# Loading the first slice of X in whole rows, and closing slice 0 in another order, in a matmul backward kernel

## The chip, the cores and the metric

One core of a Trainium2 chip. The metric is the device time of one execution in microseconds (us); all executions below count as undisturbed (fast). Verdicts come with a 95% interval. A profile is of one execution: of the kernel before a further one. Its span (first to last instruction) is about 1.8 us shorter than the device time.

## The reference

```python
batch, m, k, n = 16, 512, 1024, 768        # float32 inputs
grad_weight = np.einsum('bmk,bmn->kn', input, grad_output)   # out: 1024 x 768, float32
```

Seen as two matrices X (8192 x 1024) and G (8192 x 768) it is out = X^T G, a sum over 8192 rows. The kernel takes them in 64 slices of 128 rows.

## The kernel before

Each slice costs TensorE twelve matmuls with 512 moving columns: part A (row groups 0 to 3 of the output, columns 0 to 511), part B (row groups 4 to 7, same columns) and part N (the last 256 columns, "narrow", in transposed form). Each part holds four PSUM banks while it is open. `ORDER` says up to which slice each part goes next, and `!` that its banks are then emptied into SBUF:

```python
ORDER = (
    "A1! N1 B2! N2 A2 N3! A3 B3 A4! B5 N5 B6! N7 A6 N8! A9! B10 N9 B12! N12! A12! "
    "B15 AB17! n17! AB26! n26! AB41! n41! AB47 A50! B50! N64!"
).split()
WARMUP = [512] * 9 + [128] * 3
```

Slice 0 comes as float32 by the hardware queues of SP and ACT and is rounded to bf16 by VectorE and ScalarE. All other slices come by the software queue of GpSimd, which rounds on the way:

```python
nc.sync.dma_start(out=gf[:, 0:NA], in_=G[0:P, 0:NA])      # NA = 512, P = 128
nc.scalar.dma_start(out=xf[:, 0:NA], in_=X[0:P, 0:NA])
nc.sync.dma_start(out=gf[:, NA:N], in_=G[0:P, NA:N])
nc.scalar.dma_start(out=xf[:, NA:K], in_=X[0:P, NA:K])
# ... (warm-up matmuls on a constant, sizes from WARMUP)
for s in range(1, S):
    gt = xg.tile([P, N], bf16, name="gt")
    xt = xg.tile([P, K], bf16, name="xt")
    nc.gpsimd.dma_start(out=gt, in_=G[s * P : (s + 1) * P, :])
    nc.gpsimd.dma_start(out=xt, in_=X[s * P : (s + 1) * P, :])
# ... (casts of slice 0, 256 columns each, alternating VectorE and ScalarE)
# at the end, for each row group k of the output:
W = NB if k < 6 else c1 - c0                               # NB = 256
for c in range(c0, c1, W):
    nc.sync.dma_start(out=OUT[:, k, c : c + W], in_=acc[:, k, c : c + W])
```

Of the kernel before, what the change touches and what calls it, by code (L numbers as in the profile page):

```python
# [8 lines left out]
P = 128  # L9
NA = 512  # L10
# [4 lines left out]


ORDER = (
    "A1! N1 B2! N2 A2 N3! A3 B3 A4! B5 N5 B6! N7 A6 N8! A9! B10 N9 B12! N12! A12! "
    "B15 AB17! n17! AB26! n26! AB41! n41! AB47 A50! B50! N64!"
).split()  # L20

WARMUP = [512] * 9 + [128] * 3
XBUFS = 42


# [1 line left out]
def kernel(  # L27
# [6 lines left out]
    nc = tc.nc  # L34
# [3 lines left out]
    B, M, K = input.shape  # L38
    _, _, N = grad_output.shape
    S = B * M // P  # L40
    KS = K // P
    NB = N - NA
# [3 lines left out]
    X = input.rearrange("b m k -> (b m) k")  # L46
# [15 lines left out]
    xs = [None] * S  # L62
# [7 lines left out]
    xf = head.tile([P, K], f32, name="xf")  # L70
    gf = head.tile([P, N], f32, name="gf")
    nc.sync.dma_start(out=gf[:, 0:NA], in_=G[0:P, 0:NA])
    nc.scalar.dma_start(out=xf[:, 0:NA], in_=X[0:P, 0:NA])
    nc.sync.dma_start(out=gf[:, NA:N], in_=G[0:P, NA:N])
    nc.scalar.dma_start(out=xf[:, NA:K], in_=X[0:P, NA:K])


    ones = nc.const_aps.tensor(1.0, (P, P), bf16)
    wps = psum.tile([P, NA], f32, name="bank7")
    for i, cols in enumerate(WARMUP):  # L80
        nc.tensor.matmul(  # L81
# [18 lines left out]
    g0 = head.tile([P, N], bf16, name="g0")  # L100
    gwide[0] = g0[:, 0:NA]
    gnarrow[0] = g0[:, NA:N]
    QX = 256

    def round_pair(dst, src, c):
        nc.vector.tensor_copy(out=dst[:, c : c + QX], in_=src[:, c : c + QX])  # L106
        nc.scalar.copy(out=dst[:, c + QX : c + 2 * QX], in_=src[:, c + QX : c + 2 * QX])  # L107

    round_pair(g0, gf, 0)
    round_pair(xs[0], xf, 0)  # L110
    nc.vector.tensor_copy(out=g0[:, NA:N], in_=gf[:, NA:N])
    round_pair(xs[0], xf, NA)

    def add_out(dst, src):
        nc.vector.tensor_add(out=dst, in0=src, in1=dst)  # L115
# [7 lines left out]
    def wide_mm(bank, k, s, start, stop, c0=0, c1=NA):  # L123
        nc.tensor.matmul(  # L124
            bank, xs[s][:, k * P : (k + 1) * P], gwide[s][:, c0:c1], start=start, stop=stop
        )
# [90 lines left out]
    for a in range(P // SQ):  # L217
        c = NA + a * NT * SQ
        nc.scalar.dma_start(
            out=rows_of[:, :, c : c + NT * SQ],  # L220
            in_=turned[a * SQ : (a + 1) * SQ].rearrange("p b r t -> p b (r t)"),
# [3 lines left out]
    for k in range(KS):  # L225
        slices = range(parts["A" if k < KS // 2 else "B"].done, S)
        pieces = [(0, NA)] if k < KS - 1 else [(0, 256), (256, 384), (384, NA)]
        for c0, c1 in pieces:
            name = free.pop(0)
            bank = psum.tile([P, NA], f32, name=name)[:, 0 : c1 - c0]  # L230
            for s in slices:
                wide_mm(bank, k, s, s == slices[0], s == slices[-1], c0, c1)
            add_out(acc[:, k, c0:c1], bank)
            free.append(name)
            W = NB if k < 6 else c1 - c0
            for c in range(c0, c1, W):
                nc.sync.dma_start(out=OUT[:, k, c : c + W], in_=acc[:, k, c : c + W])

# [29 lines left out]
```

## Time and profile before

| | before |
|---|---|
| median time of 3 runs | 176.31 us (176.06 to 176.32) |
| span of the profile | 174.5 us |
| TensorE busy | 98% of the span |
| slice 1 begins on TensorE | 8.15 us |

The lines that show what bounds the kernel stand in the prediction. The columns are start, duration, engine, line, operation, tiles and count, then the idle time ahead and what ended it.

Weight loads run ahead of the matmuls, so where a load waits the matmuls themselves stand still for 0.33 us less than the load, by the start times of the matmuls in the trace. The difference of 0.33 us is the same at all such places below.

### The profile page before, as it was taken

Reading aid. Unit: us, or ns where it says so; the run is one execution under the profiler, and the core shown is the slowest. Engines: PE = TensorE matmul, PEld = TensorE weight load, DVE = VectorE, ACT = ScalarE, POOL = GpSimd, SP = SyncE. Lnnn points to the kernel's source line nnn. Section 1 sums busy time; section 2 is a strip of 40 time slices with the busy share of each in tenths; the row PEclk is TensorE's granted clock in tenths of the full one; section 3 lists DMA queues with packets and bytes.
Section 4 is the critical chain, followed back from the end, with each engine's and each line's share of the span. In section 5 each row is a group of like instructions: output and inputs, shape, how many; then the busy total and the mean of one; then the engine's idle time right before and its main releaser. Section 6 shows DMA issues by size and latency. Waiting matters only on the chain.

```text
span 174.5 us, 2024 instructions
## 1 busy us (share of the span) xinstructions
PE 170.8 (98%) x808; PEld 78.2 (45%) x808; DVE 60.8 (35%) x100; ACT 5.6 (3%) x10; POOL 66.9 (38%) x130
## 2 busy tenths in 40 slices
PE   8999999999999999999999999999999999999993
PEld 3344444444444444444444444444444444444463
DVE  0555582882940039300000662200460003932122
ACT  3440000000000000000000000000000000000000
POOL 7444444444434444444444444444174300000000
PEclk9999999999999999999999999999999999999999
DMA  5999999999999999999999999999999990085633
GB/s 160 231 208 207 208 209 208 209 208 208 209 210 208 208 208 209 208 209 208 208 208 208 210 209 206 209 207 208 208 209 208 207 206 16 0 190 149 168 98 120
DMA packets 25192, 33.09 MB, mean 190 GB/s; under 512 B 6496, under 2 KB 16608, under 8 KB 25184
## 3 DMA queue, kind: packets, MB, share of 16 engines
q0 software_dynamic: 18144, 28.91, 90.6%
q1 hardware_dynamic: 2592, 2.49, 4.3%
q10 hardware_dynamic: 4448, 1.57, 4.0%
q8 instruction: 6, 0.10, 0.2%
q14 instruction: 2, 0.02, 0.0%
HBM read 58.72 MB, written 3.15 MB: 355 GB/s over the span
## 4 chain that ended last, share of the span: by engine, by line
PE 94%; DMA 4%; issue 0%; POOL 0%; DVE 0%; POOLq 0%
PE bank L124 63%; PE bank L131 31%; DMA xt<-in_input_dram 4%; POOL gt L93 0%; DVE acc L115 0%; POOLq L252 0%
## 5 line engine op out<-in xcount | busy, mean ns | idle before, releaser
L124 PE MATMUL bank<-gt,xt 128*128 128x512 bf16 (+2 forms) x532 | 111.0, 368 | 0.1
L124 PEld LDWEIGHTS <-xt 128*128 128x128 bf16 x532 | 50.8, 98 | 58.8 <-DMA xt<-in_input_dram 1.1
L115 DVE TENSOR_TENSOR acc<-bank,acc 128x512 f32<-128x512 f32 (+2 forms) x62 | 37.9, 667 | 73.5 <-PE bank L124 73.1
L131 PE MATMUL bank<-xt,gt 128*128 128x512 bf16 x252 | 56.2, 379 | 0.0
L94 POOL DMA_DIRECT2D xt<-in_input_dram x63 | 33.5, 531 | 41.3 <-DMA xt<-in_input_dram 38.3
L93 POOL DMA_DIRECT2D gt<-in_grad_output_dram x63 | 33.6, 533 | 29.4 <-DMA gt<-in_grad_output_dram 26.9
L131 PEld LDWEIGHTS <-gt 128*128 128x128 bf16 x252 | 24.6, 98 | 29.8
L115 DVE TENSOR_TENSOR acct<-bank,acct 128x512 f32<-128x512 f32 x24 | 15.7, 682 | 30.0 <-PE bank L131 29.9
L81 PE MATMUL bank<-const-bfloat16-1.0 128*128 128x512 bf16 (+1 forms) x12 | 4.3, 550 | 0.8 <-PEq L252 0.8
L119 DVE COPY acc<-bank 128x512 f32<-128x512 f32 x4 | 2.6, 684 | 1.5 <-PE bank L124 1.5
L81 PEld LDWEIGHTS <-const-bfloat16-1.0 128*128 128x128 bf16 x12 | 1.6, 144 | 3.2 <-issue 3.2
L175 DVE STREAM_TRANSPOSE turned<-acct 128x512 f32<-128x512 f32 x4 | 2.9, 714 | 0.1
L124 PE MATMUL bank<-g,x 128*128 128x512 bf16 x8 | 2.4, 430 | 0.0
L121 ACT COPY acc<-bank 128x512 f32<-128x512 f32 x4 | 2.1, 589 | 1.8 <-PE bank L124 1.8
L106 DVE CAST g<-gf 128x256 bf16<-128x256 f32 x1 | 0.3, 324 | 4.3 <-DMA gf<-in_grad_output_dram 4.3
L119 DVE COPY acct<-bank 128x512 f32<-128x512 f32 x2 | 1.3, 686 | 1.3 <-PE bank L131 1.3
L107 ACT ACT_TABLE_LOAD x1 | 1.3, 1283 | 1.7 <-PEq L252 1.7
L124 PEld LDWEIGHTS <-x 128*128 128x128 bf16 x8 | 0.8, 108 | 1.1 <-ACT x L107 0.3
L121 ACT COPY acct<-bank 128x512 f32<-128x512 f32 x2 | 1.1, 588 | 1.5 <-PE bank L131 1.5
L131 PE MATMUL bank<-x,g 128*128 128x512 bf16 x4 | 1.0, 379 | 0.0
L107 ACT CAST x<-xf 128x256 bf16<-128x256 f32 x2 | 0.8, 402 | 0.5 <-DMA xf<-in_input_dram 0.5
L106 DVE CAST x<-xf 128x256 bf16<-128x256 f32 x2 | 0.6, 287 | 0.3 <-DMA xf<-in_input_dram 0.3
(7 smaller groups left out, 1.5 us busy)
## 6 DMA issues: line engine op xcount, KB each, us to landing
xt<-in_input_dram POOLq DMA_DIRECT2D x63, 256.0 KB, 8.5
gt<-in_grad_output_dram POOLq DMA_DIRECT2D x63, 192.0 KB, 8.5
out_dram<-acc SPq DMA_DIRECT2D x13, 128.0 KB, 2.9
out_dram<-turned ACTq DMA_DIRECT2D x4, 256.0 KB, 3.4
xf<-in_input_dram ACTq DMA_DIRECT2D x2, 256.0 KB, 4.1
gf<-in_grad_output_dram SPq DMA_DIRECT2D x1, 256.0 KB, 3.6
out_dram<-acc SPq DMA_DIRECT2D x1, 256.0 KB, 2.0
gf<-in_grad_output_dram SPq DMA_DIRECT2D x1, 128.0 KB, 3.8
```

Of the source, the lines that this page charges most:

```text
L81: nc.tensor.matmul(wps[:, 0:cols], ones, nc.const_aps.tensor(1.0, (P, cols), bf16), start=True, stop=True,)
L93: nc.gpsimd.dma_start(out=gt, in_=G[s * P : (s + 1) * P, :])
L94: nc.gpsimd.dma_start(out=xt, in_=X[s * P : (s + 1) * P, :])
L106: nc.vector.tensor_copy(out=dst[:, c : c + QX], in_=src[:, c : c + QX])
L107: nc.scalar.copy(out=dst[:, c + QX : c + 2 * QX], in_=src[:, c + QX : c + 2 * QX])
L115: nc.vector.tensor_add(out=dst, in0=src, in1=dst)
L119: nc.vector.tensor_copy(out=dst, in_=src)
L121: nc.scalar.copy(out=dst, in_=src)
L124: nc.tensor.matmul(bank, xs[s][:, k * P : (k + 1) * P], gwide[s][:, c0:c1], start=start, stop=stop)
L131: nc.tensor.matmul(bank, gnarrow[s].rearrange("p (r t) -> p t r", t=NT)[:, t], xs[s][:, h * NA : (h + 1) * NA], start=start, stop=stop,)
L175: nc.vector.transpose(out=turned[:, h * hb : (h + 1) * hb, :, t], in_=dst.rearrange("p (b r) -> p b r", r=SQ),)
```

## The change

X of slice 0 comes in one transfer of whole rows (4 KB) rather than two of half rows, with wide and then narrow G beside it on the other hardware queue. Slice 0 is worked off in the order A, B, N rather than A, N and B later. The casts are cut so that the first weights are ready soonest, the warm-up is 0.32 us longer to meet the later start, and output row group 6 goes out in two pieces.

```diff
-    "A1! N1 B2! N2 A2 ...
+    "A1! B1 N1 B2! N2 A2 ...
-WARMUP = [512] * 9 + [128] * 3
+WARMUP = [512] * 10 + [128] * 2
-    nc.scalar.dma_start(out=xf[:, 0:NA], in_=X[0:P, 0:NA])
+    nc.scalar.dma_start(out=xf, in_=X[0:P, :])
     nc.sync.dma_start(out=gf[:, NA:N], in_=G[0:P, NA:N])
-    nc.scalar.dma_start(out=xf[:, NA:K], in_=X[0:P, NA:K])
 # ... cut: the old casts, 256 columns each
+    round_by("DVE", g0, gf, 0, 256)
+    round_by("ACT", g0, gf, 256, NA)
+    round_by("DVE", xs[0], xf, 0, P)
+    round_by("ACT", xs[0], xf, 2 * P, 4 * P)
+    round_by("DVE", xs[0], xf, P, 2 * P)
+    round_by("DVE", xs[0], xf, 4 * P, 6 * P)
+    round_by("ACT", xs[0], xf, 6 * P, 8 * P)
+    round_by("DVE", g0, gf, NA, N)
-            W = NB if k < 6 else c1 - c0
+            W = NB if k < 7 else c1 - c0
```

More of the change, by code (lines that the diff above doesn't have):

```diff
@@ L17 @@
 ORDER = (
-    "A1! N1 B2! N2 A2 N3! A3 B3 A4! B5 N5 B6! N7 A6 N8! A9! B10 N9 B12! N12! A12! "
+    "A1! B1 N1 B2! N2 A2 N3! A3 B3 A4! B5 N5 B6! N7 A6 N8! A9! B10 N9 B12! N12! A12! "
     "B15 AB17! n17! AB26! n26! AB41! n41! AB47 A50! B50! N64!"
 ).split()
-WARMUP = [512] * 9 + [128] * 3
+WARMUP = [512] * 10 + [128] * 2
 XBUFS = 42
@@ L102, with round_by @@
     gnarrow[0] = g0[:, NA:N]
-    QX = 256
-    def round_pair(dst, src, c):
-        nc.vector.tensor_copy(out=dst[:, c : c + QX], in_=src[:, c : c + QX])
-        nc.scalar.copy(out=dst[:, c + QX : c + 2 * QX], in_=src[:, c + QX : c + 2 * QX])
-    round_pair(g0, gf, 0)
-    round_pair(xs[0], xf, 0)
-    nc.vector.tensor_copy(out=g0[:, NA:N], in_=gf[:, NA:N])
-    round_pair(xs[0], xf, NA)
+    def round_by(engine, dst, src, c0, c1):
+        copy = nc.vector.tensor_copy if engine == "DVE" else nc.scalar.copy
+        copy(out=dst[:, c0:c1], in_=src[:, c0:c1])
+    round_by("DVE", g0, gf, 0, 256)
[6 more added lines that the diff above has]
+    round_by("DVE", g0, gf, NA, N)
     def add_out(dst, src):
```

## The prediction

> **What bounds the kernel now.** I read the page first (busy shares, then the chain that ended last), then that chain in order of time, then the timeline of the first 9 us, and last the DMA view in windows of 1 us over the same stretch.
>
> ```profile
> PE 170.8 (98%) x808; PEld 78.2 (45%) x808; DVE 60.8 (35%) x100; ACT 5.6 (3%) x10; POOL 66.9 (38%) x130
> ...
> PE 94%; DMA 4%; issue 0%; POOL 0%; DVE 0%; POOLq 0%
> ```
>
> The reader is to see that TensorE carries 94% of the chain. The work is 64 slices of 12 matmuls with 512 moving columns, 768 in all (28 more instructions only come from cutting the last group in three). In the chain by time, four of them take 0.86 us, so one takes 0.216 us and 768 take 165.8 us. The span is 174.5 us. So all that a change of the beginning can touch is the 8 us ahead of the steady stream.
>
> ```profile
> 1.89 6.22 DMA xt<-in_input_dram
> 8.11 0.05 issue
> 8.15 1.04 PE bank L124 x4
> ```
>
> This is the head of the chain by time. After 8.15 us it is matmuls all the way to 171.71 us (163.6 us for the 756 matmuls of slices 1 to 63). What sets 8.15 us is the landing of X of slice 1, a transfer of the software queue that was issued at 1.89 us. Slice 0 itself is not on the chain.
>
> ```profile
> 4.91 0.13 PEld L124 LDWEIGHTS <-x 128*128 128x128 bf16 x2
> ...
> 5.32 0.15 PEld L124 LDWEIGHTS <-x 128*128 128x128 bf16 x1 [0.28 <-ACT x L107]
> 5.54 0.40 ACT L107 CAST x<-xf 128x256 bf16<-128x256 f32 x1 [0.50 <-DMA xf<-in_input_dram]
> ...
> 5.71 0.10 PEld L124 LDWEIGHTS <-x 128*128 128x128 bf16 x1 [0.24 <-issue]
> ...
> 8.15 0.55 PEld L124 LDWEIGHTS <-xt 128*128 128x128 bf16 x4 [0.61 <-DMA xt<-in_input_dram]
> ```
>
> The timeline shows the slack. Slice 0 starts at 4.92 us. Its first two matmuls take about 0.40 us each (weights at 4.91, 5.32, 5.71), the rest 0.216 us; the twelfth starts at 7.65 us, so TensorE could take slice 1 at 7.87 us. It takes it at 8.15 us. The gap that slice 1 causes is thus only 0.28 us (the 0.61 us in the row is the weight load's, which runs ahead).
>
> ```profile
> DMA packets 293, 0.38 MB, mean 377 GB/s; under 512 B 45, under 2 KB 173, under 8 KB 293
> ...
> q10 hardware_dynamic: 120, 0.21, 56.3%
> q1 hardware_dynamic: 173, 0.16, 47.5%
> ...
> q0 software_dynamic: 83, 0.13, 69.9%
> q10 hardware_dynamic: 94, 0.16, 41.9%
> ```
>
> These are the DMA view's windows 3.5 to 4.5 us (first three lines) and 4.5 to 5.5 us (last two). Slice 0 comes by q1 (G, from SP) and q10 (X, from ACT). The software queue q0 moves nothing until 4.5 us, though its first transfer was issued at 1.23 us. In the single packet records q0 starts on a DMA engine 6 ns after the last hardware packet there (hardware done at 4.589, 4.764, 4.817 us; software packets at 4.595, 4.770, 4.823 us). The last hardware packet of X's second half is at 5.15 us. From there slice 1 needs 8 packets of G at 135 ns and 8 of X at 173 ns on an engine, 2.46 us; its last packet of X was at 7.76 us and TensorE started 0.39 us later. So **slice 1 lands about 3.0 us after slice 0's slowest DMA engine is done**, and that is the quantity the change can move.
>
> **What the Trainium skill says.** "TensorE: Matmul & The Clock Gate", Part 1, section "Wait — 56ns, not 53.3ns?": 512 columns take 426.7 ns on the cold and 215.7 ns on the warm clock. The trace agrees: the warm-up loads stand 0.427 us apart, the stream's matmuls 0.216 us. The same page, "What's actually happening", says that warming takes a stretch of time, not a number of matmuls; here the second real matmul takes 0.39 us, so the clock turned at about 5.67 us. "DMA: Bandwidth & Descriptors", section "Queues, rings and completion order", says an engine goes round its queues packet by packet. The trace agrees for q1 and q10, and contradicts it for q0, which waits until both are empty. The same page, "Anatomy of one DMA", puts most of a transfer's fixed cost of about 2 us on the receipt of the last byte; here last packet to first dependent instruction is only 0.39 us (5.15 to 5.54).
>
> **The change part by part.**
>
> *X of slice 0 in one transfer.* It removes 128 packets of the 512 of slice 0 (rows of 4 KB in place of two of 2 KB). A 2 KB packet takes 84 ns and a 1 KB packet 46 ns in the records, so about 8 ns is fixed, and eight packets saved on an engine are 0.07 us. More may come from the slow start: in the windows view the DMAs move 184, 229 and 295 GB/s in the half microseconds from 2.0 to 3.5 us, against 355 to 400 later, with a busy share down to 0.71. If that is the pace at which row descriptors are made, twice the bytes in each would fill the engines earlier, worth at best 0.4 us. I take 0.2 us for the two together: slice 0's slowest engine done at 4.95, slice 1 at TensorE at 7.95 us.
>
> *A later start of slice 0.* The first half of X let casts start at 4.58 us; the whole of X can only be used when all of it has landed. The second half was usable at 5.54 us; narrow G is now behind it in q1 rather than between, and the rows are longer, so I expect X at about 5.1 us. The first weight cast is now 128 columns, an estimate of 0.2 us from 0.28 us for 256. First matmul at about 5.3 us, against 4.92. The longer warm-up (one 512 for one 128: +0.32 us) would end at 5.21 us, just before that, so it costs nothing.
>
> *What the later start costs TensorE.* Until 5.67 us the clock is cold and a matmul costs 0.427 in place of 0.216 us, so waiting there loses only half. Twelve matmuls from S end at 5.67 + 12 x 0.2157 - 0.505 x (5.67 - S). For S = 4.92 this gives 7.88 (the trace: 7.87). For S = 5.3 it gives 8.07 us.
>
> *Order A, B, N.* Six casts become eight, two of them of 128 columns; all fit. B needs the last X cast 0.9 us after the first, and its weights are wanted 1.3 us after the first matmul. N takes the banks that A frees: VectorE copies the first after its casts, around 6.7 us, N asks at about 7.2 us; the third bank is free near 7.4, asked at 7.6. This is the tightest place, with 0.2 us to spare.
>
> *Tail.* Row group k = 6 goes out in two transfers of 256 columns instead of one of 512. They are issued at about 169.3 and 169.7 us, ahead of the last group's issues (170.6, 171.3, 172.05). The last transfer still ends the run: 0.
>
> *Sum.* Slice 1 starts at the later of 8.07 (TensorE) and 7.95 us (landing): 8.07 against 8.15, so -0.08 us. The 163.6 us of stream and the tail stay. 176.31 - 0.08 = about 176.2 us.
>
> **The rivals.** (a) *Slice 0 takes the wait's place.* X lands as late as the second half did, 5.5 us; the first matmul is at 5.8, TensorE is done with slice 0 at 8.3: +0.15 to +0.25 us, 176.5. For it: a transfer's end is that of its slowest engine, and the engines' ends were spread over 0.55 us. Against it: narrow G, not X, should now be last. (b) *The longer rows speed nothing.* The slow start is latency of the first packets (some of 300 to 700 ns in the records) and not a pace of descriptors. Slice 1 still lands at 8.15 us and the time is the same, 176.3. (c) *The full gain.* The engines are full from 2.5 us, X lands at 4.8, the warm-up alone sets the start at 5.21: 8.03, 176.2; the landing at 7.75 is then no limit. (d) *A bank wait* before N, if narrow G lands after 6 us and holds VectorE's queue: +0.2 to +0.4 us.
>
> **Range and chances.** All of these lie within half a microsecond of 176.3, and the runs of before spread over 0.26 us. Range 175.85 to 176.6 us. A 2% change would be 3.5 us, half of all that lies ahead of the stream: faster 0.01, same 0.98, slower 0.01.
>
> **What would show it.** Right: the first real matmul at 5.2 to 5.4 us; q0's first packets at 4.4 to 4.6; the first weight load of slice 1 at 8.0 to 8.1 with almost no DMA wait ahead of it; 163.6 us after it as before. Wrong: a wait of several tenths on X at the first weight load (rival a), the same wait on slice 1 of about 0.3 us (b), a wait of N's first or third matmul on a bank copy (d), or any gap after 8.2 us. My least certain number is the 0.2 us that slice 0's transfers gain.

## More of the kernel before

```profile
30.73 0.55 PEld L124 LDWEIGHTS <-xt 128*128 128x128 bf16 x4 [0.45 <-DMA xt<-in_input_dram]
```

This is TensorE's first weight load from slice 11. It stood waiting until X of that slice had landed.

## The result, and the profile after

| | before | changed |
|---|---|---|
| median time, 4 runs each | 176.31 us (176.06 to 176.51) | 176.31 us (176.09 to 176.73) |
| ratio | | 1.0003 (0.9979 to 1.0028): same |
| span of the profile | 174.5 us | 175.0 us |

Ratios here are the mean time of one kernel's runs over that of the other's of the same rounds, so not quite the ratio of the medians quoted.

The time is the same. The profiled execution of the changed kernel was its slowest (176.73 us), which has to be kept in mind when the two profiles are laid side by side.

The timeline of the changed kernel, at the places shown of the kernel before (line numbers have moved by two):

```profile
5.11 0.67 DVE L105 CAST x<-xf 128x128 bf16<-128x128 f32 x3
5.37 0.10 PEld L126 LDWEIGHTS <-x 128*128 128x128 bf16 x1 [0.22 <-DVE x L105]
...
6.20 0.15 PEld L126 LDWEIGHTS <-x 128*128 128x128 bf16 x1 [0.28 <-issue]
...
6.56 0.74 PEld L126 LDWEIGHTS <-x 128*128 128x128 bf16 x4 [0.21 <-issue]
...
8.29 0.74 PEld L126 LDWEIGHTS <-xt 128*128 128x128 bf16 x4
...
31.18 0.55 PEld L126 LDWEIGHTS <-xt 128*128 128x128 bf16 x4 [0.56 <-DMA xt<-in_input_dram]
```

Three things are to be seen. Slice 0 starts at 5.37 us in place of 4.92. The weight loads stay about 0.4 us apart until 6.56 us, so TensorE's clock was still on half speed then; in the profile of before it had turned at 5.67 us. (The column of the granted clock says 1.00 throughout; only the spacing shows it.) And there is no wait at slice 1 any more (8.29 us), but the wait at slice 11 is longer, 0.23 us of standing matmuls in place of 0.12.

The DMA view of the changed kernel in the windows 3.5 to 4.5 us (first three lines) and 4.5 to 5.5 us (last three):

```profile
DMA packets 190, 0.39 MB, mean 394 GB/s; under 512 B 30, under 2 KB 90, under 8 KB 190
...
q10 hardware_dynamic: 74, 0.25, 62.3%
q1 hardware_dynamic: 114, 0.14, 37.6%
...
q0 software_dynamic: 110, 0.17, 100.8%
q1 hardware_dynamic: 84, 0.07, 20.9%
q10 hardware_dynamic: 4, 0.00, 0.2%
```

Slice 0 comes faster, as hoped: the last hardware packet starts at 4.90 us in place of 5.15, and the software queue begins at 4.42 in place of 4.60 us. But the windows view shows what became of that (columns: window, length, busy time of PE, PEld, DVE, ACT and POOL, clock, DMA share, GB/s), first before, then changed:

```profile
5.50:6.00 0.50, 0.50 (x4) 0.17 (x2) 0.46 (x2) 0.46 (x2) 0.10 (x1) 1.00 1.16 200
6.00:6.50 0.50, 0.50 (x4) 0.22 (x3) 0.50 (x2) 0.50 (x2) 0.00 (x0) 1.00 1.11 201
```

```profile
5.50:6.00 0.50, 0.50 (x2) 0.23 (x2) 0.48 (x3) 0.33 (x2) 0.10 (x1) 1.00 1.23 127
6.00:6.50 0.50, 0.50 (x2) 0.15 (x1) 0.48 (x1) 0.05 (x1) 0.02 (x1) 1.00 0.59 111
```

The software queue moved 127 and 111 GB/s where it had moved 200. In the packet records seven of the first packets of X of slice 1 took 0.68 to 0.95 us each; the usual is 0.17 us. X of slice 1 landed at 8.23 us, against 8.11 before: the head start was lost before slice 1 was in. That the slow packets are the reason is likely, but not shown: in the table below one profile with three of them (before, slice 11 later) has X of slice 1 at 7.80 us.

The chain that ended last of the changed kernel, by time, no longer begins with slice 1:

```profile
21.74 9.40 DMA xt<-in_input_dram
31.14 0.05 issue
31.18 1.04 PE bank L126 x4
```

It ends its DMA part at X of slice 11. The last matmul starts at 171.48 us before and at 171.93 us changed. Counted from the first matmul of slice 11 (30.73 and 31.18 us) that is 140.75 us in both.

### The profile page after: what moved, and what is told of

The parts are those of the page before. It is cut to its first block, busy times and chain, and to the rows that moved or that the text cites. A ratio compares the mean times of both kernels' runs of the same rounds, so it can differ in the third digit from the quotient of the medians. Undisturbed runs are those within 1.5% of the kernel's fastest.

```text
span 175.0 us, 2010 instructions
## 1 busy us (share of the span) xinstructions
PE 170.5 (97%) x793; PEld 78.4 (45%) x808; DVE 61.1 (35%) x101; ACT 5.6 (3%) x10; POOL 66.9 (38%) x130
## 4 chain that ended last, share of the span: by engine, by line
PE 80%; DMA 15%; POOL 2%; issue 1%; DVE 0%; POOLq 0%
PE bank L126 53%; PE bank L133 27%; DMA xt<-in_input_dram 15%; POOL gt L92 1%; POOL xt L93 1%; DVE acc L117 0%; POOLq L254 0%
## 5 line engine op out<-in xcount | busy, mean ns | idle before, releaser
L133 PEld LDWEIGHTS <-gt 128*128 128x128 bf16 x252 | 24.7, 98 | 29.7
L105 DVE CAST x<-xf 128x128 bf16<-128x128 f32 (+1 forms) x3 | 0.7, 342 | 0.0
```

Source lines behind the costliest of these rows:

```text
L105: copy(out=dst[:, c0:c1], in_=src[:, c0:c1])
L133: nc.tensor.matmul(bank, gnarrow[s].rearrange("p (r t) -> p t r", t=NT)[:, t], xs[s][:, h * NA : (h + 1) * NA], start=start, stop=stop,)
```

## The experiments

Two theories to start with. **Two limits:** the end is the later of two chains, TensorE's start of slice 1 (163.2 us to the start of the last matmul follow) and the landing of X of slice 11 (140.75 us follow). **The start alone:** whatever moves the beginning of slice 1 moves the end, and the wait at slice 11 is incidental.

The times of each group of runs are set beside runs of the kernel before on the same chip in the same rounds. A table of all profiles is at the end of this section.

### Both kernels again (two runs)

No edit.

> The changed kernel, unaltered, for repeats and a second profile. Theory (two limits): the end is set by the later of TensorE's start of slice 1 (about 163.3 us of stream follow) and the landing of X of slice 11 near 31 us (about 140.8 us follow). 176.1 to 176.5 us; first real matmul 5.3 to 5.4 us; hardware queues empty at 4.9 us; X of slice 1 lands 7.9 to 8.2 us if the slow first packets of the first profile were chance, 8.2 again if they belong to the change. Rival (start alone): no wait for slice 11 in this profile.

> The kernel before, unaltered, for a second profile. Theory: first real matmul at 4.9 us; hardware queues empty at 4.9 to 5.2 us; slice 1 begins at 8.1 us with a wait if the clock turns early, at 8.25 us without one if it turns after 6.4 us; 176.05 to 176.5 us. Rival (landing of slice 1 alone): slice 1 always begins after a wait.

The changed kernel: 176.22 us (five runs, 176.04 to 176.54) beside 176.16 us, ratio 1.0001 (0.9988 to 1.0015). The kernel before: 176.13 us (two runs) beside 176.21 us of its other runs. The profiles, taken with the first ones, show what varies from one execution to the next. The clock turned at about 6.6 us in the second profile of the changed kernel; in the second of the kernel before it had turned before slice 0 began. And X of slice 11 landed at 30.33 us in the former (no wait), where it had been 31.14. Its chain therefore consists of TensorE alone:

```profile
0.78 4.64 PE bank L80 x12
5.41 2.44 PE bank L126 x8
7.86 0.86 PE bank L133 x4
8.72 0.86 PE bank L126 x4
```

The kernel before in turn started slice 1 at 7.86 us (8.1 was expected), 0.29 us sooner than in its first profile, and waited longer at slice 11 (0.21 us), so that 0.20 us of the 0.29 were left at the end. The rival's expectation of the changed kernel (no wait at slice 11) was met in this one profile but not in the first; which chain is the longer one changes from execution to execution.

### X in one transfer, alone

```diff
 (kernel before)
-nc.scalar.dma_start(out=xf[:, 0:NA], in_=X[0:P, 0:NA])
+nc.scalar.dma_start(out=xf, in_=X[0:P, :])
-nc.scalar.dma_start(out=xf[:, NA:K], in_=X[0:P, NA:K])
```

> The kernel before with X of slice 0 in one transfer and nothing else of the change (order A, N, B, casts of 256 columns, short warm-up). Theory: hardware queues empty at 4.9 us in place of 5.15, first real matmul at 5.4 to 5.5 us (cast of 256 columns after X at 5.1), slice 1 then started with little or no wait at 8.1 to 8.5 us by the clock's turn; 176.3 to 176.6 us. Rival (longer rows speed nothing): hardware queues empty at 5.15 us again, first matmul at 5.8 or later, 176.6 or more.

176.58 us (four runs, 176.04 to 176.69) beside 176.16, ratio 1.0017 (1.0001 to 1.0032). The profile met the expectation on the beginning: hardware queues done at 4.97 us, first matmul at 5.42, slice 1 at 8.02. But that execution was the fast one of the four (176.04, the clock had turned before slice 0 began); why the other three took 0.5 to 0.65 us more no profile shows.

### Slice 11 wanted later (two runs)

```diff
-... A9! B10 N9 B12! N12! A12! ...
+... A9! B10 N9 B11 N10 B12! N12! A12! ...
```

> The changed kernel with the order B10 N9 B11 N10 B12 N12 A12 in place of B10 N9 B12 N12 A12: TensorE wants slice 11 four matmuls (0.86 us) later, same work. Theory (two limits): the wait for X of slice 11 (0.23 us in the first profile) is gone and the time falls by 0.1 to 0.25 us to about 176.1. Rival (the start alone sets the end): the same time as the changed kernel, no wait there in either.

> The kernel before with the same change of order. Theory (two limits): its wait for X of slice 11 (0.12 us) goes, the time falls by 0.1 to 176.2 us, and the start of slice 1 (8.15 us, set by the landing of X of slice 1) is then the only limit. Rival: unchanged 176.3.

Changed kernel with this order: 176.18 us beside 176.22 unaltered and 176.16 before (ratio to before 1.0001, 0.9989 to 1.0014). Kernel before with this order: 176.09 beside 176.16, ratio 0.9998 (0.9985 to 1.0010). The waits at slice 11 are gone in both profiles, but no gain shows in the times. The intervals, about 0.2 us to either side, do not exclude the 0.1 us expected of the kernel before, nor a small gain of the changed kernel, so these two runs decide nothing between the theories by their times. Their profiles say a little more: TensorE stood nowhere after slice 1, and the last matmul started 163.2 us after slice 1 began (8.13 and 8.29 us, the latter because the clock turned only at about 6.5 us), so in these two executions the first chain was the longer. The next place that could bind is seen in the profile of the changed kernel with the new order, a weight load that arrives just as its data does:

```profile
41.72 3.21 PEld L126 LDWEIGHTS <-xt 128*128 128x128 bf16 x16 [0.24 <-DMA xt<-in_input_dram]
```

This is slice 16. Its X landed at 41.68 us; the load waited 0.24 us, less than the 0.33 us by which it runs ahead, so the matmuls lost nothing, but there was little slack either.

### One transfer more on the software queue, long after the start (two runs)

```diff
 (changed kernel)
 for s in range(1, S):
+    if s == 9:
+        nc.gpsimd.dma_start(out=spare, in_=G[0:P, 0:NA])   # read by nobody
```

alone, and together with the order of the last experiment.

> The changed kernel with one more transfer on the software queue, ahead of slice 9 (512 columns of G of slice 0 again, into a tile that nobody reads): by the packets about 0.7 us of the DMA engines, long after slice 1 began. Theory (two limits): X of slice 11 lands 0.7 us later (31.1 to 31.8 us), TensorE waits 0.4 to 0.9 us for it and the time rises by 0.4 to 0.8 us though the start is untouched. Rival (the start alone sets the end): unchanged, the wait is absorbed.

> The same extra transfer with slice 11 wanted 0.86 us later (the order of the second experiment). Theory (two limits): the slack takes the extra transfer, no wait above 0.2 us at slice 11, time within 0.15 us of the changed kernel. Rival (an extra transfer costs its time wherever it lies): plus 0.7 us as without the new order.

Alone: 176.82 us beside 176.18 (ratio 1.0031, 1.0016 to 1.0046), 0.6 us more, as two limits expected and the start alone did not. With the later slice 11: 176.90 us (ratio 1.0043, 1.0027 to 1.0058), where two limits expected the slack to absorb it. The rows of the weight loads that waited show why; first without, then with the new order:

```profile
31.71 0.55 PEld L129 LDWEIGHTS <-xt 128*128 128x128 bf16 x4 [1.33 <-DMA xt<-in_input_dram]
```

```profile
31.61 0.54 PEld L129 LDWEIGHTS <-xt 128*128 128x128 bf16 x4 [0.42 <-DMA xt<-in_input_dram]
40.43 1.41 PEld L129 LDWEIGHTS <-xt 128*128 128x128 bf16 x8 [0.51 <-DMA xt<-in_input_dram]
42.65 3.14 PEld L129 LDWEIGHTS <-xt 128*128 128x128 bf16 x16 [0.81 <-DMA xt<-in_input_dram]
```

Without it TensorE stands 1.00 us at slice 11. With it it stands 0.10 us at slice 11, then 0.18 at slice 15 and 0.48 at slice 16. The wait was not removed but handed on. So it is not one landing but **the pace of the software queue** over the first 42 us that forms the second chain: a slice lands every 2.2 us (slice 9 apart, see the table below), TensorE needs 2.59 us for twelve matmuls but wants new slices early because of the order of the parts, and the schedule is so tight that slices 1, 11 and 16 each arrive about when they are wanted. This is shown for an added delay. That the small waits of the unaltered kernels would all reappear at slice 16 is only likely.

### TensorE starts later (two runs)

```diff
 (changed kernel)            -WARMUP = [512] * 10 + [128] * 2   +WARMUP = [512] * 12 + [128] * 2
 (kernel before)             -WARMUP = [512] * 9 + [128] * 3    +WARMUP = [512] * 11 + [128] * 3
```

> The changed kernel with two more warm-up matmuls of 512 columns: TensorE gets to slice 0 only at about 6.06 us (5.37 at the soonest in the changed kernel) while no transfer moves. Theory (TensorE's own start and the turn of its clock set when slice 1 begins; the landing of X of slice 1 at 8.1 us has at most 0.4 us on it): slice 1 begins at 8.65 us when the clock turns early, 8.9 us when late, and the time rises by 0.35 to 0.5 us. Rival (the landings of slices 1 and 11 alone set the end): unchanged.

> The kernel before with the same two more warm-up matmuls: slice 0 from 5.75 us in place of 4.92. Theory: slice 1 begins at 8.35 us (clock early) to 8.7 us (late) in place of 8.15 to 8.3, so the time rises by 0.2 to 0.45 us, less than in the changed kernel, since the wait for slice 1 hides the first part. Rival (landings alone): unchanged.

The changed kernel took 176.58 us beside 176.21 (ratio 1.0020, 1.0006 to 1.0033), as expected in time; its profile is of the fastest of the five (176.33 us), and there slice 1 began at 8.26 us, not at 8.65 or later, so the expected way is not shown. The kernel before took 176.14 us (five runs, 175.98 to 176.19; ratio 0.9993, 0.9980 to 1.0005): nothing, a miss, and what the rival expected. In both profiled executions the clock turned during the warm-up (at about 5.1 us), so the first matmul came at 5.58 and 5.42 us, sooner than I had reckoned. In the kernel before slice 1 then began at 8.01 us without a wait, and slice 11 waited 0.17 us all the same. A start that is 0.5 us later is thus free in that kernel as long as the clock has turned. Whether the longer warm-up is itself why all five of its executions were fast is open; one of five was profiled.

### More on the hardware queue

```diff
 (changed kernel)
 nc.sync.dma_start(out=gf[:, NA:N], in_=G[0:P, NA:N])
+nc.sync.dma_start(out=spare, in_=G[0:P, 0:NA])             # read by nobody
```

> The changed kernel with 256 KB more on the hardware queue of SP (wide G of slice 0 once more, into a tile that nobody reads). Theory (the software queue gets a DMA engine only when the hardware queues have nothing left for it): hardware queues empty at 5.5 us in place of 4.9, first software packet at about 5.0 in place of 4.4, X of slice 1 lands at 8.7 in place of 8.1, TensorE waits for it and the time rises by 0.2 to 0.5 us. Rival (the software queue has its own delay of 2.5 us after its first issue): first software packet at 4.4 us again, interleaved with hardware packets.

177.19 us beside 176.21 (ratio 1.0054, 1.0038 to 1.0069). The first software packet was at 4.42 us, not at 5.0, and the hardware queue was busy until 7.7 us. The DMA view from 5.5 to 7.5 us:

```profile
q0 software_dynamic: 162, 0.28, 74.9%
q1 hardware_dynamic: 133, 0.25, 35.9%
```

Both queues have packets in the same stretch. So the reading of the prediction, that the software queue waits until the hardware queues are empty, falls as a rule, and what the rival expected (4.4 us, interleaved) came. What remains is that the software packets begin 6 ns after the hardware transfers' last packets, which a delay of the software queue's own would not give: in every one of the fourteen profiles, this one too, 11 to 19 of the first 40 software packets start exactly 6 ns after the 4-byte packet that closes a hardware transfer (the records do not name the engine; the pairs are matched by time). In the present run the added transfer only got going at 5.36 us, after the software queue had begun, and from then they shared. What lets the software queue begin stays open. The added time was 1.0 us, twice the most expected. Of it 0.43 us lies after the last matmul; the next experiment explains that part. The rest lies at slices 1 and 11 (8.72 and 31.48 us).

### X in halves within the changed kernel (two runs)

```diff
 (changed kernel)
-nc.scalar.dma_start(out=xf, in_=X[0:P, :])
+nc.scalar.dma_start(out=xf[:, 0:NA], in_=X[0:P, 0:NA])
 nc.sync.dma_start(out=gf[:, NA:N], in_=G[0:P, NA:N])
+nc.scalar.dma_start(out=xf[:, NA:K], in_=X[0:P, NA:K])
 second run only:  -W = NB if k < 7 else c1 - c0   +W = NB if k < 6 else c1 - c0
```

> The changed kernel with X of slice 0 in two transfers of half rows again; order A, B, N, the smaller casts, the longer warm-up and the output pieces stay. Theory: the hardware queues are empty 0.1 to 0.25 us later than with whole rows (5.0 to 5.15), but the first real matmul is not later (5.21 to 5.3 us, held by the warm-up), slice 1 begins at the same 8.1 (clock early) to 8.4 us (late): 176.0 to 176.4 us, the same. Rival (whole rows are worth something): 0.2 us more than the changed kernel.

> The changed kernel with X of slice 0 in two halves again, and row group 6 of the output in one transfer again, so that the hardware transfers are 24 as in both kernels and not 25 as in the run before this one. Theory (the 0.42 us longer tail of that run comes from the order of the last waits on the transfers' semaphores, which turns with the number of transfers, and whole rows are worth nothing): last matmul to end 3.0 us in place of 3.44, time 176.1 to 176.35 us, the same as both kernels. Rival (half rows cost 0.4 us): 176.6 us again with a tail of 3.4.

With half rows alone: 176.67 us beside 176.18 (ratio 1.0025, 1.0011 to 1.0038), against the expectation of no difference. But its stream of matmuls was not longer: the last one started at 171.36 us. The tail from there to the end of the span was 3.44 us, against 3.02. With the output piece put back as well: 176.17 us beside 176.09, ratio 1.0001 (0.9989 to 1.0013), and a tail of 3.02. The waits of SP's queue at the end show the difference, first the former run, then the latter (columns: waiter, releaser, total us, times, longest):

```profile
SPq L266 <- DMA out_dram<-acc: 1.1, 1, 1.1
```

```profile
SPq L266 <- DMA out_dram<-acc: 0.7, 1, 0.7
```

At the end SP waits for the semaphores of all queues, one after the other in a fixed order, 0.06 us each. With 24 hardware transfers (both kernels: 4 + 4 + 16 before, 3 + 4 + 17 changed, loads, transposed pieces and the rest of the output) the last transfer's semaphore stands near the end of that order. With 25 it stands near the beginning: SP waits there first, and eight checks, most of which could have been done meanwhile, follow after the landing (0.51 us to the last), where with 24 only one does (0.08 us). The run with more on the hardware queue had 25 as well and the same 3.45 us. The kernel before with X whole had 23: two checks follow, and its tail was 3.07 us. So the split of row group 6 in the change makes up for the load that was saved, but without it the count would have been 23, not 25, and 0.05 us is all that it can have saved.

The latter run also has the clearest case of a gain handed back:

```profile
7.82 0.55 PEld L127 LDWEIGHTS <-xt 128*128 128x128 bf16 x4 [0.51 <-DMA xt<-in_input_dram]
30.92 0.54 PEld L127 LDWEIGHTS <-xt 128*128 128x128 bf16 x4 [0.97 <-DMA xt<-in_input_dram]
```

Slice 1 began at 7.82 us, sooner than in any other profile here, and TensorE then stood 0.64 us at slice 11. In both runs with halves TensorE also stood 0.08 to 0.09 us at the third matmul of part N of slice 0, just after a bank copy of VectorE had ended (7.15 us, matmul at 7.20 in the former).

### All profiles in one table

Starts of matmuls and landings in us from the span's start; "stood" is TensorE's idle time at that slice, "last" the start of the last matmul, the last column the time of that execution.

| profile | X | first real | X of slice 1 landed | slice 1 begins | stood at 11 | last | us |
|---|---|---|---|---|---|---|---|
| before | halves | 4.92 | 8.11 | 8.15 | 0.12 | 171.48 | 176.27 |
| before again | halves | 4.91 | 7.82 | 7.86 | 0.21 | 171.28 | 176.06 |
| before, slice 11 later | halves | 4.89 | 7.80 | 8.29 | 0 | 171.47 | 176.26 |
| before, start later | halves | 5.42 | 7.74 | 8.01 | 0.17 | 171.37 | 176.16 |
| before, X whole | whole | 5.42 | 7.94 | 8.02 | 0 | 171.20 | 176.04 |
| changed | whole | 5.37 | 8.23 | 8.51 | 0.23 | 171.93 | 176.73 |
| changed again | whole | 5.37 | 8.07 | 8.55 | 0 | 171.74 | 176.54 |
| changed, slice 11 later | whole | 5.24 | 8.09 | 8.13 | 0 | 171.33 | 176.11 |
| changed, start later | whole | 5.58 | 8.21 | 8.26 | 0.08 | 171.54 | 176.33 |
| changed, software extra | whole | 5.37 | 8.21 | 8.26 | 1.00 | 172.46 | 177.25 |
| same, slice 11 later | whole | 5.37 | 8.15 | 8.20 | 0.10 | 172.18 | 176.96 |
| changed, hardware more | whole | 5.71 | 8.36 | 8.72 | 0.31 | 172.23 | 177.45 |
| changed, X halves | halves | 4.71 | 7.87 | 7.92 | 0.24 | 171.36 | 176.60 |
| same, 24 transfers | halves | 4.67 | 7.78 | 7.82 | 0.64 | 171.67 | 176.49 |

Where TensorE stood nowhere after slice 1, the last matmul starts 163.2 us after slice 1 begins (four profiles). Where it stood at slice 11, it starts 140.75 us after slice 11 begins (all of them but the one that stood again at slices 15 and 16). Halves land X of slice 1 at 7.74 to 8.11 us, whole rows at 7.94 to 8.36 us, though with whole rows the hardware transfers are done some 0.1 us sooner (4.84 to 4.97 us, without the one with more on that queue, against 4.90 to 5.15). First packets of X of slice 1 of over 0.6 us are found in every profile of the changed kernel with its whole rows but the one with more on the hardware queue (one to seven per profile), and in three of the six with halves (one to three). What makes them slow no experiment settled.

The table does not show one step on which slice 11 depends. In every profile X of slice 9 landed 2.67 to 3.31 us after X of slice 8 (3.6 with the added software transfer), where the steps before it took 2.15 to 2.26 us. From the landing of slice 1 to that of slice 11 it was thus 22.26 to 23.10 us in the twelve profiles without the added software transfer. This spread of 0.84 us is larger than that of the landing of slice 1 itself (7.74 to 8.36 us). So how long TensorE stands at slice 11 hangs on this uneven step, and on the catching up in the one after it (1.5 to 2.2 us), at least as much as on the start: in the profile that stood 0.64 us the step took 3.24 us, and the whole way 23.10. What makes the step long was not tested; the last point of this document has a candidate.

No variant beat both kernels: the best median, 176.09 us of the kernel before with slice 11 later, is within the interval of its own comparison.

## Why the prediction was right or wrong

The number was right: 176.2 us forecast, 176.31 measured, within the range. That says little for the way to it: by the prediction's own sums rivals (a), (b) and (c) lay within the range as well. Its steps:

- *Slice 0's transfers gain 0.2 us.* The direction held, the size only against the first profile: 4.90 us where 4.95 was forecast and 5.15 had been, and 394 GB/s from 3.5 to 4.5 us in place of 377. In the six profiles of the changed kernel with whole rows and no added hardware transfer it was 4.84 to 4.95 us, but in the six with halves 4.90 to 5.15, so that the means differ by 0.1 us. The first profile was the latest of those six.
- *"slice 1 at TensorE at 7.95 us."* This failed. X of slice 1 landed at 8.07 to 8.23 us in those profiles. The prediction carried the gain over to slice 1 by a fixed distance of 3.0 us; from the last hardware packet to the landing it was 3.2 to 3.3 us there, against 2.7 to 3.0 with halves. First packets of up to 0.95 us are the likely reason, not a shown one. The term of -0.2 us measured +0.12 us in the first pair of profiles, and +0.3 us between the means of those six profiles (8.16 us) and of the six with halves (7.85 us).
- *First matmul at about 5.3 us, warm-up not in the way.* Right: 5.37, and 5.24 in one profile. The order A, B, N and the bank copies made no wait at part N in any profile of the changed kernel with whole rows; with halves the place that the prediction called the tightest, N's third matmul, cost 0.08 to 0.09 us. (The prediction counted six casts before; there were seven.)
- *What the later start costs.* The formula holds, but it took the turn of the clock at 5.67 us for a constant. Over the profiles it lay between some 3.5 us and 6.6 us. With the turn at 6.5 us in it, it gives 8.5 us for the start of slice 1, which is what the changed kernel's profile shows (8.51). This is the largest difference between single executions at the beginning.
- *"After 8.15 us it is matmuls all the way."* This was a misreading of a merged chain: the wait at slice 11 was there. It is the reason why a head start on slice 1 buys so little: TensorE then only gets sooner to a slice that has not landed.
- *Tail: 0.* Right (3.02 and 3.03 us), but what sets the tail was not in the prediction: the count of hardware transfers, 24 in both kernels. With 23 it was 3.07 us, with 25 it was 3.44.
- *Rivals.* Of (a) a little is true (TensorE, not the landing, set slice 1 when the clock turned late), of (b) the outcome (slice 1 no sooner) but not its cause. A second bound, the software queue's pace, was missing from the list.

So the expected gain of 0.08 us was never large enough to be measured, and the larger movements under it, 0.45 us of later start and 0.1 to 0.25 us of faster transfers, were taken up by slack: the wait for slice 1 that was there before, the half-speed clock, and the software queue, whose slice 11 landed at 30.48 and 30.69 us in the two profiles of before and at 30.33 and 31.14 us in the two of the changed kernel.

## What to carry to other kernels

Before you shave a beginning, look for the next place where the same stream is waited for; a short wait 20 us later can be the twin that takes the whole gain back. A chain that is merged into long pieces hides waits of a tenth of a microsecond, so ask for the waits themselves. And when an edit changes the number of transfers, look at the tail before you judge the edit.

## What the Trainium skill lacked or had wrong

- "DMA: Bandwidth & Descriptors", section "Queues, rings and completion order", has engines go round the queues packet by packet. That agrees with hardware and software packets side by side (133 and 162 packets from 5.5 to 7.5 us in the run with more on the hardware queue), but it does not explain why in the kernel before software packets, whose transfer had been issued at 1.23 us, began only at 4.60 us, 6 ns after a hardware transfer's last packet.
- The same page, section "Anatomy of one DMA", gives a transfer of the software queue a fixed cost of about 2 us and puts most of it on the receipt of the last byte; from the last packet of X of slice 1, which came by that queue, to the first matmul on it was 0.39 us here (7.76 to 8.15). The page says nothing of slow first packets when a queue goes on to its next transfer (0.68 to 0.95 us against 0.17).
- "TensorE: Matmul & The Clock Gate", section "What's actually happening", gives the turn of the clock a spread of 500 ns to either side; here it lay between some 3.5 and 6.6 us, with the warm-up always from 0.78 us. Its other figure, 6, 11 or 14 slow matmuls from run to run of one kernel, fits better: here 6 to 15 came before the turn.
- No page has that the tail turns with the count of transfers: with 25 eight semaphore checks of 0.06 us lie after the last landing, with 24 one, which makes 0.42 us.
- "Runtime: NRT & Kernel Launch", section "Instruction fetch mechanics", has instructions fetched by DMA in blocks of 16 KiB and calls the cost mostly hidden; it says nothing of what a fetch does to transfers on other queues. One packet of 16 KB on the queue of kind "instruction" took 0.89 us at 24.1 us in the profile of before (24.7 us changed), and X of slice 9 landed 2.85 us (3.25 us) after slice 8 in place of 2.2. All fourteen profiles have such a packet at 23.8 to 24.7 us and a long step to slice 9. That the one caused the other is an inference; no run moved the fetch.
